# Experts of a two-block network in quads of 32 slots per token tile, on 32-column tiles of TensorE

## The chip, the cores and the metric

One core of one Trainium2 chip runs the whole program once. The metric is the device time of that execution in microseconds (us), the median of several runs. TensorE is called PE, VectorE DVE, ScalarE ACT, GpSimd POOL, and SyncE, whose queue issues the weight loads, SP.

## What is computed

256 tokens of width 1024 pass through two blocks. The first (attention, a short convolution and two feed-forward parts) and the mixing layers of the second are not touched by the change. Each of the two layers of the second block ends in a mixture of experts, which is:

```python
def hier_moe(x, w_group, b_group, w_router, b_router, w_gate, w_up, w_down):
    # N_GROUPS = 4, EXPERTS_PER_GROUP = 4, N_EXPERTS = 16, TOP_K_IN_GROUP = 2, D_EXPERT = 256
    probs_g = jax.nn.softmax((xf @ w_group + b_group).astype(jnp.float32), axis=-1)
    p_top, g_idx = lax.top_k(probs_g, 1)
    ...
    w_top, e_local = lax.top_k(probs_in, TOP_K_IN_GROUP)
    ids = g_idx * EXPERTS_PER_GROUP + e_local
    gates = jnp.einsum('tk,tke->te', p_top * w_top, jax.nn.one_hot(ids, N_EXPERTS, dtype=jnp.float32))
    h = jax.nn.silu(jnp.einsum('td,edf->tef', xf, w_gate)) * jnp.einsum('td,edf->tef', xf, w_up)
    y = jnp.einsum('tef,efd->td', h * gates[:, :, None].astype(h.dtype), w_down)
```

So each token takes the two best experts of its best group, and the result, added to sqrt(2) times the token, goes through a layer normalization.

## The kernel before

**Tokens and weights.** The 256 tokens are two tiles of 128, T = 0 and 1, called T0 and T1 below. All weights are streamed once: `make_plan` lists 512 KB pieces ("units", 128 x 1024 in f32) in the order in which they are used, and SP loads them through a ring of 34 tiles of that size, which also holds the split copies of the dense weights and the larger intermediate tiles (`tS`). A load waits until the last reader of the ring tile that it takes has finished. A layer's experts are 64 units of gate and up weights (`eg`, four per expert) and 32 of down weights (`ed`, two per expert), 96 in all.

**Order.** `Sched` emits the program: every part is a generator that yields the events and estimated times it waits for, and the part that can go on first is emitted next. So each engine's queue holds a fixed order, made from estimated times, and the engines then wait for each other through semaphores.

**An expert layer.** `front_half` transposes a tile and multiplies it with the router's weights. `moe_front` (one call per tile) picks the experts on DVE in some twenty small instructions (`choose`), numbers each expert's tokens by a product with a triangular matrix (the matmul `bk<-mks,cst`), and makes a selection matrix `sel` by comparing with an iota. Its slots are CAP = 64 per expert, counted over both tiles, so 16 x 64 = 1024 columns. A flag is raised if an expert got more than CAP tokens; then a second program (`moe_all`) computes everything again without slots.

`gather` forms the tokens of four experts (256 slots), transposed: per 128 of the 1024 features two tiles of tokens times two parts of a two-part split (`xs`), each a product with 256 columns of `sel`; then `affine` applies the gain and the bias of the normalization, on ACT and DVE by turns. It is called four times.

`moe_task` then goes through the experts in eight pairs, `pr`. `gate_up(pr)` multiplies the 64 slots of each expert of the pair with its gate and up weights (512 columns), in plain f32, the two experts side by side in two 64-column tiles of PE; each such product is two PE instructions in the profile. `slot_gates` (twice) brings the gate of each slot to its partition (`gsl`), and the gate is multiplied into the hidden values. `transposed` turns these, `down(pr-1)` multiplies the previous pair's with its down weights, one bank per half of the 1024 columns, and splits the result `ys` in two parts (ACT cast, DVE subtract). `combine(pr-2)` adds it to the four output banks `out` by products with the transposed selection `selT`: two tiles, two column halves, two parts, so eight products of 512 columns per pair. For pairs 4 and 5 the residual sqrt(2) x is added in the same banks through the identity. `moe` then takes the normalization's statistics from the banks.

Of the kernel before, what the change touches and what calls it, by code (L numbers as in the profile page):

```python
# [22 lines left out]
CAP = 64  # L23
# [7 lines left out]
# ---------------------------------------------------------------- host layout  # L31
# [28 lines left out]
class Plan:  # L60
    """The order in which pieces of the weights are loaded."""
# [11 lines left out]
def make_plan(again=False):  # L73
# [3 lines left out]
    def put(name, kind, n):  # L77
        ids.setdefault(name, [])
        for _ in range(n):
            i = len(ids[name])  # L80
            ids[name].append(p.add(kind, (name, i)))
# [29 lines left out]
    if again:  # L111
        for nm, kd in (moe(0) + lnrows("f0") + [("bin", "dense")] * 20 + [("wo1", "dense")] * 8 + lnrows("m1")
                       + moe(1) + lnrows("f1")):
            put(nm, kd, 1)
        return p, ids
# [20 lines left out]
    for nm, kd in moe(0)[:12] + lnrows("m0") + moe(0)[12:]:  # L136
        put(nm, kd, 1)
# [4 lines left out]
    for nm, kd in moe(1)[:12] + lnrows("m1") + moe(1)[12:]:  # L142
        put(nm, kd, 1)
    for nm, kd in lnrows("f1"):
        put(nm, kd, 1)
    return p, ids


def host_arrays(inp):
# [3 lines left out]
    for i in range(2):  # L153
# [10 lines left out]
        u[f"eg{i}"] = eg.reshape(8, 2, 4, 128, 1024).transpose(0, 2, 1, 3, 4).reshape(64, 128, 1024)  # L164
        ed = np.stack([_down_block(g["w_down_2"][i][e]) for e in range(NEXP)])
        u[f"ed{i}"] = ed.reshape(8, 2, 2, 128, 1024).transpose(0, 2, 1, 3, 4).reshape(32, 128, 1024)
# [62 lines left out]
C_N = 516 + 64  # L229
# [59 lines left out]
class Body:  # L289
# [68 lines left out]
    # ---- estimates of when the vector and scalar engines are done  # L358
# [23 lines left out]
    # ---- small helpers  # L382
# [55 lines left out]
    def mm(self, out, lhsT, rhs, start, stop, shared=False):  # L438
# [72 lines left out]
    # ---- weights  # L511
# [104 lines left out]
    # ---- pieces  # L616
    def setup(self):
# [39 lines left out]
        self.gsl = c.tile([128, 8], F32, name="gsl")  # L657
        self.flag = c.tile([128, 2], F32, name="flag")
# [11 lines left out]
    def gate(self, i):  # L670
        """Until everything before piece i that is not of its own line has been taken."""
# [9 lines left out]
    def ada_task(self):  # L681
        for i in range(2):
            order = [(j, (b,)) for b in range(2) for j in (1, 0)] if i == 0 else [(1, (0, 1)), (0, (0, 1))]
            for j, halves in order + [(j, (0, 1)) for j in (2, 4, 3, 5)]:
# [20 lines left out]
                for b in halves:  # L705
                    d = dst[:, b * 512:(b + 1) * 512] if dst is not None else None
                    if onpe:
                        yield [self.gate(uid[4 * b + 3]), self.unit(uid[4 * b + 3]), self.bk(1)] + ([] if gate else [self.rH(1)])
                        bank = self.bank()
                        for q in range(4):  # L710
                            raw = self.take(uid[4 * b + q]).rearrange("p (k n) -> p k n", k=2)
                            for kk in range(2):
# [3 lines left out]
                                self.sch.now -= 0.22  # L716
# [48 lines left out]
    def gemm(self, T, uids, lhs, blocks, n=512, tail=None, ev=None):  # L765
        """Token-major product of a 128-token tile with streamed weights, one block of columns after another."""
# [29 lines left out]
    def gemm_halves(self, T, uids, lhs, blocks, ev):  # L796
        """As gemm, all the blocks with the first half of the rows before the second half."""
# [21 lines left out]
    def lhsT(self, T, src, out, dst=None, cols=None, at=(0.0, 0.0)):  # L819
        """Transposes [128, 1024] and splits it into two parts, in two halves; cols: a factor and a term per column."""  # L820
# [53 lines left out]
    def residual(self, T, acc, c, g):  # L874
        """x += g * acc on the columns c."""
# [6 lines left out]
    # ---- memory keys and values  # L882
# [46 lines left out]
    def mem_attention(self, T, layer, qm, mm):  # L929
        """qm: [128, 256] on chip. Writes the last two pieces of the mixed tokens, both parts of them."""  # L930
# [54 lines left out]
    # ---- block 1, layer 0  # L985
# [113 lines left out]
    # ---- feed-forward  # L1099
# [52 lines left out]
    # ---- block 1, layer 1  # L1152
# [85 lines left out]
    # ---- block 2  # L1238
# [12 lines left out]
    def residual_half(self, T, b, acc):  # L1251
        """x = alpha x + y on half of the columns, and what its mean and variance take."""
# [13 lines left out]
    def affine_rows(self, T, nm, src):  # L1266
        """x = (src - mean) rstd gain + bias."""
# [13 lines left out]
    def affine_pool(self, T, nm, src):  # L1281
        """The same on the other engines."""
# [534 lines left out]
    def moe_front(self, T, layer):  # L1817
# [29 lines left out]
        if T == 0:  # L1847
            bank = self.bank()
# [357 lines left out]
```

## Time and profile before

| | us |
|---|---|
| median of 3 runs (1238.99 to 1245.82) | 1243.78 |
| span of the profiled execution | 1241.5 |
| PE busy | 1185.2 (95%) |
| DVE busy | 735.7 (59%) |
| ACT busy | 548.4 (44%) |
| mean granted TensorE clock (1 is 2.4 GHz) | 0.980 |
| bytes read from HBM | 299.05 MB, 243 GB/s over the span |

The profiled execution is known by its span, from its first to its last instruction; the median of the runs is 2.3 us longer. Busy shares are averages over stages with different limits. The two expert layers lie at about 824 to 957 us and 1095 to 1228 us of the span, and the stages are read from the views of these stretches. A row of the timeline gives the start, the time from the first start to the last end of merged instructions, engine, line, operation, names, count, and in brackets the idle time before with what ended it.

### The profile page before, as it was taken

What the parts mean: (1) busy time and instruction counts of PE and PEld (TensorE: products, weight loads), DVE (VectorE), ACT (ScalarE), POOL (GpSimd) and SP (SyncE); (2) the same over time, 40 slices, a digit from 0 to 9 for tenths busy, and PEclk for the clock granted to TensorE, in tenths of its full rate; (3) what the DMA queues carried; (4) which work ended last, traced back from release to release, by engine and by line L of the source; (5) the groups of instructions that cost most, each with busy time, mean ns of one, the idle gap of its engine ahead of it and who ended that gap; (6) DMA issues with size and microseconds to landing.
All of it is one profiled execution on the core that took longest, in us unless ns stands there. A gap on an engine that the chain in (4) does not pass through costs nothing. (4 is left out here: it accounts for less than half of the span.)

```text
span 1241.5 us, 15838 instructions
## 1 busy us (share of the span) xinstructions
PE 1185.2 (95%) x5892; PEld 874.0 (70%) x5892; DVE 735.7 (59%) x1177; ACT 548.4 (44%) x912; POOL 45.2 (4%) x60
## 2 busy tenths in 40 slices
PE   7999999999989999999999999989998999899995
PEld 5777778888867887888887798765443786675432
DVE  4477667766768886555657567773313755564213
ACT  4565564534455556433445845422211566422211
POOL 0021000000000000000000001000000100000001
PEclk9999999999999999999999999989999899889998
DMA  9986768677766765556663323857999332487991
GB/s 378 408 283 231 277 219 294 243 260 268 278 229 234 278 228 174 211 208 208 209 211 106 118 86 125 313 206 279 394 408 360 139 133 101 156 325 288 410 409 42
DMA packets 83540, 301.87 MB, mean 243 GB/s; under 512 B 9408, under 2 KB 9824, under 8 KB 83456
## 3 DMA queue, kind: packets, MB, share of 16 engines
q1 hardware_dynamic: 82224, 298.39, 65.9%
q0 software_dynamic: 944, 2.02, 0.5%
q8 instruction: 48, 0.79, 0.3%
q10 hardware_dynamic: 288, 0.38, 0.1%
q14 instruction: 36, 0.29, 0.1%
HBM read 299.05 MB, written 2.10 MB: 243 GB/s over the span
## 5 line engine op out<-in xcount | busy, mean ns | idle before, releaser
L439 PE MATMUL bk<-hi,tS 128*128 128x512 f32 (+1 forms) x1760 | 585.8, 399 | 13.0 <-ACT hi L493 9.4
L439 PEld LDWEIGHTS bk<-hi,tS 128*128 128x128 f32 x1760 | 332.7, 190 | 88.9 <-ACT hi L493 10.0
L474 DVE TENSOR_TENSOR lo<-raw,hi 128x1024 fp32r<-128x1024 f32 x266 | 316.3, 1220 | 54.3 <-ACT hi L493 53.1
L439 PE MATMUL bk<-lo,tS 128*128 128x512 f32 (+1 forms) x880 | 344.5, 391 | 1.8 <-DVE lo L474 1.8
L493 ACT CAST hi<-raw 128x1024 fp32r<-128x1024 f32 x262 | 262.8, 1048 | 6.6 <-DMA raw<-in_units_dram 6.4
L439 PEld LDWEIGHTS bk<-lo,tS 128*128 128x128 f32 x880 | 167.5, 190 | 34.7 <-DVE lo L474 3.1
L467 ACT ACTIVATE tH<-bk 128x256 f32<-128x256 f32 (+1 forms) x94 | 42.2, 451 | 237.2 <-PE bk L439 237.1
L439 PE MATMUL bk<-hi,tH 128*128 128x512 f32 x384 | 132.8, 396 | 0.0
L439 PE MATMUL bk<-raw,tB 128*64 128x512 f32 x384 | 87.0, 602 | 0.0
L439 PEld LDWEIGHTS bk<-hi,tH 128*128 128x128 f32 x384 | 72.5, 189 | 15.0 <-issue 0.2
L474 DVE TENSOR_TENSOR tS<-bk,tS 128x512 fp32r<-128x512 f32 (+2 forms) x58 | 35.9, 633 | 70.2 <-ACT tS L493 68.9
L439 PE MATMUL bk<-raw,tH 128*64 128x512 f32 x320 | 74.5, 597 | 1.2 <-ACT tH L493 1.2
L439 PE MATMUL bk<-lo,tH 128*128 128x512 f32 x192 | 75.0, 391 | 0.0
L493 ACT CAST tS<-bk 128x512 fp32r<-128x512 f32 (+1 forms) x60 | 31.8, 544 | 92.3 <-PE bk L439 72.5
L485 DVE SCALAR_TENSOR_TENSOR tS<-raw,cs,tS 128x1024 f32<-128x1024 f32 x52 | 66.5, 1278 | 0.2
L439 PE MATMUL bk<-tS 128*128 128x256 f32 (+2 forms) x316 | 62.3, 342 | 0.0
L439 PEld LDWEIGHTS bk<-raw,tB 128*64 128x64 f32 x384 | 26.4, 138 | 49.3 <-issue 46.1
L439 PEld LDWEIGHTS bk<-tS 128*128 128x128 f32 x316 | 50.3, 203 | 11.2 <-issue 6.5
L474 DVE TENSOR_TENSOR tH<-tH,bk 128x256 f32<-128x256 f32 x44 | 18.4, 419 | 63.3 <-ACT tH L467 63.2
L451 PE MATMUL bk<-identr,tH 128*128 128x128 f32 x272 | 47.3, 279 | 8.5 <-DVE tH L474 5.9
L451 PEld LDWEIGHTS bk<-identr,tH 128*128 128x128 f32 x272 | 33.8, 141 | 30.3 <-issue 10.5
L493 ACT CAST tH<-bk 128x256 fp32r<-128x256 f32 (+1 forms) x52 | 18.5, 355 | 79.6 <-PE bk L451 75.5
(189 smaller groups left out, 1037.2 us busy)
## 6 DMA issues: line engine op xcount, KB each, us to landing
raw<-in_units_dram SPq DMA_DIRECT2D x556, 512.0 KB, 5.6
row<-in_rows_dram SPq DMA_DIRECT2D x9, 512.0 KB, 6.4
x<-in_x_dram SPq DMA_DIRECT2D x2, 512.0 KB, 8.8
xsave<-x POOLq DMA_DIRECT2D x2, 512.0 KB, 9.1
out_dram<-x SPq DMA_DIRECT2D x3, 256.0 KB, 2.0
ulv<-in_ulv_dram POOLq DMA_DIRECT2D x1, 576.0 KB, 7.2
cst<-in_consts_dram SPq DMA_DIRECT2D x1, 290.0 KB, 9.7
out_dram<-x ACTq DMA_DIRECT2D x1, 256.0 KB, 2.0
```

Of the source, the lines that this page charges most:

```text
L439: self.nc.tensor.matmul(out, lhsT, rhs, start=start, stop=stop, skip_group_check=shared)
L451: self.nc.tensor.transpose(out, in_, self.ident)
L467: self.nc.scalar.activation(out, in_, func, scale=scale)
L474: self.nc.vector.tensor_tensor(out, a, b, op)
L485: self.nc.vector.scalar_tensor_tensor(out, a, s, b, op0, op1)
L493: self.nc.scalar.copy(out, a)
```

## The change

Slots are now counted per tile of tokens: CAP is 32, and `sel` of each tile has 16 x 32 = 512 columns, both tiles side by side in `ulv`. The experts go in four quads `q` instead of eight pairs, and the matmuls of a quad lie on four 32-column tiles, for each tile of tokens apart: `gate_up(q, tiles)` has 8 x 4 products per tile, `down(q, c)` 2 x 2 x 4 for one half `c` of the output columns. `gather` is one call per tile of tokens, with 512 columns and no sum over tiles, and the first quad's `gate_up` is called for T0 and T1 apart, with T1's gather between them. The gates are multiplied into the outputs of `down`, when the two parts are made (ACT copy with a scale, DVE `scalar_tensor_tensor`), and no longer into the hidden values. `combine(q, c)` has four products, since slots of one tile go to that tile alone. The plan's order is 16 units of `eg` and 8 of `ed` in turn, with the down weights laid out by column half. The estimated time of a 32-column matmul in `mm` goes from 0.53 to 0.26 of the full one (0.22 us was taken off by hand before).

```diff
-CAP = 64
+CAP = 32
...
     def moe(i):
-        g, d = [(f"eg{i}", "raw")] * 8, [(f"ed{i}", "raw")] * 4
-        return g + (g + d) * (NEXP // 2 - 1) + d
+        g, d = [(f"eg{i}", "raw")] * 16, [(f"ed{i}", "raw")] * 8
+        return g + (g + d) * (NEXP // 4 - 1) + d
...
-            c = max(0.858 * n / 512, 0.11) * (0.53 if m <= 64 else 1.0)
+            c = max(0.858 * n / 512, 0.11) * (0.26 if m <= 32 and n == 512 else 0.53 if m <= 64 else 1.0)
...
-        sel = self.tS(F32R) if T else self.ulv[:, :1024]
-        self.sel[T] = sel
-        s3 = sel.rearrange("p (e s) -> p e s", e=16)
-        for a, n in ((0, 4), (4, 12)):
-            self.tt(s3[:, a:a + n], p1[:, a:a + n].unsqueeze(2).to_broadcast([128, n, CAP]),
-                    self.cst[:, C_IOTA:C_IOTA + CAP].unsqueeze(1).to_broadcast([128, n, CAP]), ALU.is_equal)
-            if a == 0:
-                self.set(f"rt{layer}_{T}")
+        sel = self.sel[T] = self.ulv[:, T * 512:(T + 1) * 512]
+        self.tt(sel.rearrange("p (e s) -> p e s", e=16), p1.unsqueeze(2).to_broadcast([128, 16, CAP]),
+                self.cst[:, C_IOTA:C_IOTA + CAP].unsqueeze(1).to_broadcast([128, 16, CAP]), ALU.is_equal)
+        self.set(f"rt{layer}_{T}")
...
+        for dk in range(8):
+            yield [self.bk(1 if T else 4), f"rt{layer}_{T}"]
             bank = self.bank()
...
+            for p in range(2):
+                self.mm(bank, self.xs[T][p][:, dk * 128:(dk + 1) * 128], self.sel[T], p == 0, p == 1)
+            self.affine(dk % 2 == 0, self.xg[T][dk], bank, A[:, dk:dk + 1], B[:, dk:dk + 1])
+            self.free()
+            self.set(f"xg{layer}_{T}_{dk}")
+        self.fS(2)
...
+        def combine(q, c):
             for T in range(2):
...
+                if out[T][c] is None:
+                    out[T][c] = self.bank()
+                for p in range(2):
+                    self.mm(out[T][c], self.selT[:, T * 512 + q * 128:T * 512 + (q + 1) * 128],
+                            ys[q, c][p][:, T * 512:(T + 1) * 512], q == 0 and p == 0, q == 3 and p == 1)
...
             self.act(h[:, :256], acc[:, :256], AF.Silu)
-            self.stt(h[:, :256], h[:, :256], gsl[:, pr:pr + 1], acc[:, 256:], ALU.mult, ALU.mult)
...
+            self.tt(h[:, :256], h[:, :256], acc[:, 256:], ALU.mult)
...
+                    for T in tiles:
+                        for e in range(4):
+                            self.mm(acc[T][32 * e:32 * e + 32], self.xg[T][k][:, (4 * q + e) * CAP:(4 * q + e + 1) * CAP],
+                                    ws[e][:, j], k == 0, k == 7)
...
             for j in range(2):
...
+                for T in range(2):
+                    for e in range(4):
+                        self.mm(y[T][32 * e:32 * e + 32], hTs[q][:, T * 256 + j * 128 + 32 * e:T * 256 + j * 128 + 32 * e + 32],
+                                ws[e][:, j * 512:(j + 1) * 512], j == 0, j == 1)
...
+                self.act(ys[q, c][0][:, n], y[T], AF.Copy, scale=g)
+                self.stt(ys[q, c][1][:, n], y[T], g, ys[q, c][0][:, n].bitcast(F32), ALU.mult, ALU.subtract)
...
         yield from self.gather(layer, 0)
...
+        yield from gate_up(0, (0,))
+        yield from self.gather(layer, 1)
+        self.SMIN = SM1
+        yield from gate_up(0, (1,))
+        yield from slot_gates()
+        yield from gate_up(1, (0, 1))
...
+        for q in range(4):
+            if q == 3:
+                self.hold = True
+            yield from down(q, 0)
+            if q > 1:
+                yield from combined(q - 1, 1)
+            yield from down(q, 1)
+            yield from combined(q, 0)
+            if q < 2:
+                yield from gate_up(q + 2, (0, 1))
+            if q == 0:
+                yield from combined(0, 1)
+                yield from residual(0)
+                yield from residual(1)
...
+        yield from combined(3, 1)
```

On PE, at the start of the first expert layer, the order before was as follows. `wr` is the router's product (T1's second half here), `mks` the products that number the tokens, `ulv` and `tS` with 256 columns the gather with T0's and T1's selection, and `raw` the expert weights.

```order
L439 MATMUL bk<-wr,tS 128x20 x4
L439 MATMUL bk<-ulv,tS 128x256 x4
L439 MATMUL bk<-mks,ones 128x16
L439 MATMUL bk<-ulv,tS 128x256 x12
L439 MATMUL bk<-mks,cst 128x16
L439 MATMUL bk<-mks,ones 128x16 x2
L439 MATMUL bk<-tS 128x256 x16
L439 MATMUL bk<-raw,tB 64x512 x12
L439 MATMUL bk<-raw,mkT_117 64x512 x2
L439 MATMUL bk<-raw,tH 64x512 x2
```

In the changed kernel the same place on PE reads:

```order
L452 MATMUL bk<-wr,tS 128x20 x4
L452 MATMUL bk<-ulv,tS 128x512 x16
L452 MATMUL bk<-mks,cst 128x16
L452 MATMUL bk<-raw,tB 32x512 x8
L452 MATMUL bk<-mks,ones 128x16 x2
L452 MATMUL bk<-raw,tB 32x512 x24
L452 MATMUL bk<-ulv,tS 128x512 x6
L464 MATMUL bk<-identr,ulv 128x128 x4
L464 MATMUL bk<-identr,tH 128x128 x2
L452 MATMUL bk<-ulv,tS 128x512 x10
```

A whole first pass over the quad's weights, for T0, now stands ahead of T1's gather; T1's pass over the same weights follows these rows.

On DVE, in the same place, T1's experts were chosen and its selection made before in this order (`mks` is the choice, `tS<-x_83,tS` the second part of T1's split, `tm<-bk,mks` the slot numbers, the two `tS<-tm,cst` T1's selection, and what follows starts the gates):

```order
L474 TENSOR_TENSOR mks<-chosen_88 128x16
L474 TENSOR_TENSOR mks<-mks,chosen_88 128x16
L474 TENSOR_TENSOR tS<-x_83,tS 128x1024
L485 SCALAR_TENSOR_TENSOR tm<-bk,mks 128x16
L474 TENSOR_TENSOR tS<-tm,cst 128x256
L474 TENSOR_TENSOR tS<-tm,cst 128x768
L481 TENSOR_SCALAR tm<-chosen_87 128x4
```

And now:

```order
L487 TENSOR_TENSOR mks<-chosen_88 128x16
L487 TENSOR_TENSOR mks<-mks,chosen_88 128x16
L487 TENSOR_TENSOR tS<-x_83,tS 128x1024
L494 TENSOR_SCALAR tB<-bk,vecs 128x512 x4
L498 SCALAR_TENSOR_TENSOR tm<-bk,mks 128x16
L487 TENSOR_TENSOR ulv<-tm,cst 128x512
L494 TENSOR_SCALAR tm<-chosen_87 128x4
```

DVE's four pieces of T0's gather stand between the choice and the slot numbers of T1.

On PE, the last rows of the first expert layer were (`tH` with `raw` is `down`, `tS` with 512 columns `combine`, `identr,tH` the transposes of hidden values, `tH,cst` and `tH,ones` the next router's):

```order
L439 MATMUL bk<-tS 128x512 x8
L439 MATMUL bk<-raw,tH 64x512 x8
L451 MATMUL bk<-identr,tH 128x128 x2
L439 MATMUL bk<-raw,tH 64x512 x8
L439 MATMUL bk<-tS 128x512 x16
```

and are now:

```order
L464 MATMUL bk<-identr,tH 128x128 x4
L452 MATMUL bk<-raw,tH 32x512 x16
L452 MATMUL bk<-tS 128x512 x4
L452 MATMUL bk<-raw,tH 32x512 x16
L452 MATMUL bk<-tS 128x512 x4
L452 MATMUL bk<-raw,tH 32x512 x16
L452 MATMUL bk<-tS 128x512 x4
L452 MATMUL bk<-raw,tH 32x512 x16
L452 MATMUL bk<-tS 128x512 x8
```

The last two quads' down products, which take 16 units, stand together at the end.

## Rows read from the trace of the kernel before

**Rows 1.** Stretches of both expert layers: busy time of each engine, clock, DMA share, GB/s

```profile
834.40:956.50 122.10, 121.51 (x602) 56.38 (x602) 38.28 (x91) 26.21 (x50) 1.69 (x3) 0.99 0.92 358
1106.10:1227.40 121.30, 120.65 (x601) 55.89 (x600) 37.28 (x88) 26.23 (x50) 0.00 (x0) 1.00 0.79 308
```

**Rows 2.** PE's timeline over one settled pair of experts, first layer

```profile
922.09 0.44 PE L451 MATMUL bk<-identr,tH 128*128 128x128 f32 x2
922.46 5.37 PE L439 MATMUL bk<-raw,tB 128*64 128x512 f32 x24
...
929.48 2.11 PE L439 MATMUL bk<-tS 128*128 128x512 f32 x8
931.52 3.65 PE L439 MATMUL bk<-raw,tH 128*64 128x512 f32 x16
935.10 0.44 PE L451 MATMUL bk<-identr,tH 128*128 128x128 f32 x2
```

**Rows 3.** PE's timeline from the first gather to the second, first layer

```profile
824.38 0.72 PE L439 MATMUL bk<-ulv,tS 128*128 128x256 f32 x4
...
828.66 0.40 PE L439 MATMUL bk<-mks,cst 128*128 128x16 f32 x2 [1.92 <-DVE mks L474]
...
830.76 3.76 PE L439 MATMUL bk<-tS 128*128 128x256 f32 x16
834.45 6.40 PE L439 MATMUL bk<-raw,tB 128*64 128x512 f32 x24
...
842.50 0.28 PE L439 MATMUL bk<-gtr,ulv 128*128 128x32 f32 x1
...
843.41 0.72 PE L439 MATMUL bk<-ulv,tS 128*128 128x256 f32 x4
...
847.27 1.03 PE L451 MATMUL bk<-identr,ulv 128*128 128x128 f32 x8
```

**Rows 4.** PE's timeline: the layers' last combines, and the second layer's start

```profile
952.72 3.93 PE L439 MATMUL bk<-tS 128*128 128x512 f32 x16
...
1093.23 0.96 PE L439 MATMUL bk<-wr,tS 128*128 128x20 f32 x8
...
1106.17 5.37 PE L439 MATMUL bk<-raw,tB 128*64 128x512 f32 x24
...
1223.45 3.92 PE L439 MATMUL bk<-tS 128*128 128x512 f32 x16
```

**Rows 5.** PE's timeline around eight products on 32-column tiles, first block

```profile
24.20 1.92 PE L439 MATMUL bk<-raw,cs 128*32 128x512 f32 x16
26.05 0.50 PE L439 MATMUL bk<-hi,tS 128*128 128x512 f32 x1
```

**Rows 6.** The weight loads into PE (PEld) of these products

```profile
24.65 0.13 PEld L439 LDWEIGHTS bk<-raw,cs 128*32 128x32 f32 x4 [0.30 <-issue]
25.08 0.13 PEld L439 LDWEIGHTS bk<-raw,cs 128*32 128x32 f32 x4 [0.30 <-issue]
```

**Rows 7.** Stretches of 5 us, busy times of instructions on `raw`; last: clock, DMA share, GB/s

```profile
830.00:835.00 5.00, 0.55 (x2) 0.30 (x4) 0.00 (x0) 0.00 (x0) 0.50 0.00 0
...
900.00:905.00 5.00, 2.12 (x10) 0.48 (x8) 0.00 (x0) 0.00 (x0) 1.00 1.03 409
```

**Rows 8.** DMA issues from 830 to 842 us: count, KB each, median us to landing

```profile
raw<-in_units_dram SPq DMA_DIRECT2D x4, 512.0 KB, 4.7
```

**Rows 9.** The page's DMA issues, over the whole span

```profile
xsave<-x POOLq DMA_DIRECT2D x2, 512.0 KB, 9.1
```

**Rows 10.** DVE's timeline in T1's front, first layer

```profile
824.58 0.80 DVE L481 TENSOR_SCALAR x<-x,stat 128x1024 f32<-128x1024 f32 x1
...
828.53 1.22 DVE L474 TENSOR_TENSOR tS<-x,tS 128x1024 fp32r<-128x1024 f32 x1
...
834.48 1.44 DVE L481 TENSOR_SCALAR tB<-bk,vecs 128x256 f32<-128x256 f32 x3
```

**Rows 11.** DVE's timeline after the last combine of the second layer

```profile
1226.05 1.30 DVE L2070 BATCH_NORM_STATS2 tm<-bk 128x6 f32<-128x512 f32 x2 [1.15 <-PE bk L439]
```

More of the change, by code (lines that the diff above doesn't have):

```diff
@@ L657, in setup @@
         self.gsl = c.tile([128, 8], F32, name="gsl")
+        self.gsw = c.tile([128, 2, 32], F32, name="gsw")
+        self.own4 = c.tile([128, 4], F32, name="own4")
+        nc.gpsimd.memset(self.own4, 0.0)
+        for q in range(4):
+            nc.gpsimd.memset(self.own4[32 * q:32 * q + 32, q:q + 1], 1.0)
         self.flag = c.tile([128, 2], F32, name="flag")
@@ L1998, in down, with gate_up @@
-        def down(pr):
-            ud = self.ids[f"ed{layer}"][4 * pr:4 * pr + 4]
-            yield [f"hT{layer}_{pr}", self.rS(2), self.bk(2)]
+            self.set(f"hT{layer}_{q}_{T}")
+        def gate_up(q, tiles):
+            ug = self.ids[f"eg{layer}"][16 * q:16 * q + 16]
+            yield [self.bk(len(tiles)), self.rH(len(tiles))]
+            acc = {T: self.bank() for T in tiles}
+            for k2 in range(4):
+                units = ug[4 * k2:4 * k2 + 4]
+                yield [self.unit(u) for u in units] + ([f"xg{layer}_{tiles[-1]}_{2 * k2 + 1}"] if q == 0 else [])
+                ws = [self.take(u).rearrange("p (k n) -> p k n", k=2) for u in units]
+                for j in range(2):
+                    k = 2 * k2 + j
+                    for T in tiles:
+                        for e in range(4):
+                            self.mm(acc[T][32 * e:32 * e + 32], self.xg[T][k][:, (4 * q + e) * CAP:(4 * q + e + 1) * CAP],
+                                    ws[e][:, j], k == 0, k == 7)
+                    if j == 0:
+                        yield 0.0
+                if tiles[-1] == 1:
+                    for u in units:
+                        self.done(u)
+            for T in tiles:
+                self.sch.spawn(hidden(q, T, acc[T]), 1.9)
@@ L2015, in down, with combined @@
+            if c:
+                self.fH()
+            for T in range(2):
+                n = slice(T * 512, (T + 1) * 512)
+                g = gsl[:, 4 * T + q:4 * T + q + 1]
+                self.act(ys[q, c][0][:, n], y[T], AF.Copy, scale=g)
+                self.stt(ys[q, c][1][:, n], y[T], g, ys[q, c][0][:, n].bitcast(F32), ALU.mult, ALU.subtract)
                 self.free()
-            self.set(f"y{layer}_{pr}")
+            self.set(f"y{layer}_{q}_{c}")
+        def combined(q, c):
+            yield [f"y{layer}_{q}_{c}"] + ([f"selT{layer}_0", f"selT{layer}_1", self.bk(2)] if q == 0 else [])
+            combine(q, c)
@@ new lines, in moe_task @@
+        yield from gate_up(0, (0,))
[4 more added lines that the diff above has]
+        yield from gate_up(1, (0, 1))
+        if layer == 0:
+            self.sch.spawn(self.router(1), 2.5)
+        for q in range(4):
+            if q == 3:
+                self.hold = True
[10 more added lines that the diff above has]
+                yield from residual(1)
@@ L2052, in moe_task @@
         self.fB()
-        yield f"y{layer}_7"
-        self.out = out
-        combine(7)
-        self.fS(2)
+        yield from combined(3, 1)
+        self.fS()
     def moe(self, T, layer):
@@ L2063, in moe @@
         yield from self.moe_front(T, layer)
-        yield f"moe{layer}_{T}"
-        if T == 1 and not self.last[T]:
-            yield lambda: self.tD - 0.3
-        acc = self.out[T]
         st = self.tm(12)
         for b in range(2):
+            yield f"moe{layer}_{T}_{b}"
+            if T == 1 and not self.last[T]:
+                yield lambda: self.tD - 0.3
+            acc = self.out[T]
             self.nc.vector.bn_stats(st[:, 6 * b:6 * b + 6], acc[b])
```

263 lines of the change are left out of this document (94 added, 169 removed).

## The prediction

> **What bounds the kernel now.** I read the stretches first, then PE's timeline, then the loads and DVE in the places that the change touches. Over the expert part of each layer PE is busy for 121.5 of 122.1 and 120.7 of 121.3 us, at a clock of 0.99 and 1.00, while DVE and ACT are busy for 38 and 26 us of it [rows 1]. A busy PE need not be at its pace, so look at one settled pair: `gate_up` takes 922.46 to 929.48, 7.02 us for 32 instructions (0.219 each), combine 2.04, `down` 3.58, the transposes 0.37, and the next pair follows at once [rows 2]. So PE sets the pace. The second limit is close behind: from 900 us the loads move 409 GB/s at a DMA share of 1.03 [rows 7], so a unit of 0.524 MB costs 1.28 us. A pair takes 12 units, 15.4 us of loads, in 13.0 us of PE: PE lives on what was loaded ahead. The loads stand still at 830 to 835 us (0 GB/s, the ring is full), where the clock is also at 0.50, its 1.2 GHz level [rows 7], after PE had waited 1.92 us for DVE's choice of T1's experts [rows 3].
>
> **The change part by part.**
>
> *The products themselves: no gain.* A pass for one tile of tokens over a quad has 32 products, 64 instructions. The eight 32-column products of the first block take 1.85 us for 16 instructions with both edges, 0.116 each [rows 5], and their weight loads come four per 0.43 us, 0.108 each [rows 6]. I take 0.108 and 0.1 us for a group's edges: 6.9 us for a pass, 3.6 for the 32 instructions of a `down`. Per layer that is 8 x (6.9 + 3.6) = 84 us, where 8 x (7.02 + 3.58) = 85 were. The bounds are 0.108 and 0.219 (the pace of 64 columns, if no more than two tiles ran at once); I stay at the row that has 32-column tiles.
>
> These rows show four tiles at once. The Trainium skill, "TensorE: Matmul & The Clock Gate", Measured speedup vs the span model, gives 2.38 times for three 32-column tiles, and its section The mechanism lets weight loads overlap running matmuls only where the row group differs, which is not so here. By 2.38 of 3 an instruction would take 0.108 x 3 / 2.38 = 0.136 us, an estimate from that page, and the layer 21 us more. The row decides.
>
> *Gather.* Four calls of 3.86 us [rows 3], 15.4, become 32 products of 512 columns at the combine's 0.24 (3.93 for 16, [rows 4]): 7.7. *Combine.* Eight of 2.04 become eight of four products, 1.0 each: 8.3 us less. *Slot gates* are made once, 0.9 us less [rows 3], and half of sixteen transposes goes, 0.9 of about 1.9. So PE has about 18 us less per layer. Scaling outputs instead of hidden values costs nothing on the path: ACT and DVE stand idle two thirds of the time [rows 1], and each handles 16 halves of 512 columns per layer as before.
>
> *T1's front: PE is filled, DVE is later.* T0's selection has half the columns, so DVE's chain for T1 starts some 0.6 us sooner (half of the 1.22 us of 1024 elements, [rows 10]) and the split ends at 829.1, not 829.7. Then four pieces of T0's gather stand ahead of T1's slot numbers in DVE's queue. A piece of 256 columns takes 0.48 (1.44 for three, [rows 10]); for 512 it is between that and 0.96, and I take 0.70, near the statistics of 512 columns in 0.65 [rows 11]. So T1's numbers wait 2.8 us, to 831.9, and its selection is there at 832.8. Queued behind are the gates, and PE's second gather waits. But PE has the first pass meanwhile: from the first of these pieces, 829.9, to 837.1 with the numbering products. Second gather and six transposes, 4.5, and edges: T1's pass begins at 841.9. In the second layer I count from the router's first half at 1093.23 [rows 4]: both router halves 1.9, transposes 0.5, gather 3.8, pass 6.9, numbering 0.3, gather 3.8, transposes 0.7, and an estimated 1.2 of waits for DVE's last pieces, which stand behind T1's choice: 1112.3. Before, the first pair began at 834.45 and 1106.17 [rows 3, 4].
>
> *PE from T1's pass to the end.* Pass 6.9, gates and transposes 1.6, quad 1 13.9, two downs with transposes and a combine 8.7, quad 2 with the next router's products 14.4, combine and transposes 1.5, residual 2.0 and about 1.5 of waiting for its parts (two scaled copies and two subtractions of 1024 columns), downs and combine 8.2, quad 3 13.9, 1.5 for its hidden values, which no other work now covers, four downs 14.4 and three combines 3.0, the last splitting and combines 2.1. Sum 93.6: PE alone would end at 935.5 and, without the router, 1205.4.
>
> *The loads.* In the built order 27 units and the two rows of a normalization are placed before T0's gather, two more behind it, units 29 and 30 (from 0) wait for T1's gather, and 31 on for T1's pass, sixteen ring tiles in 7 us. So from 841.9 on the loads never wait for the ring: unit 29 lands 4.7 us later (a load into an idle queue, [rows 8]) and each further one after 1.28. The last, 95, lands at 841.9 + 4.7 + 66 x 1.28 = 931.1; the two 512 KB of `xsave` in the first layer [rows 9] take 2.6 of the same DMA: 933.7. The last `down` and the last splitting, 5.7, end at 939.4. In the second layer 1112.3 + 4.7 + 84.5 + 5.7 = 1207.2. Both are later than PE alone, by 3.9 and 1.8: **the loads become the bound, narrowly.** Before, the ends were 956.65 and 1227.37 [rows 4]. Gains 17.2 and 20.2.
>
> *Tails.* Before, T0's statistics began 1.3 us ahead of PE's last combine (1226.05 against 1227.37, [rows 4, 11]), since T0's four products came first. Now the last half of both tiles comes last and DVE has its splitting to finish first: about 1 us lost in each layer.
>
> Sum: 17.2 + 20.2 - 2 = 35.4, so a span of about 1206 for the 1241.5 of the profiled execution. The median of the runs is 2.3 above that span: **1208 us**.
>
> **The rivals.**
>
> *Loads come later still.* SP issues in order, so one ring tile freed late holds all units behind it: two units of the third quad wait for DVE's last use of the normalization's rows, and several for combines. For it: quad 3 and the last downs use 32 units in 33 us of PE, where the loads need 41. Against: by then the queue is many units behind its free tiles. If about 6 units are lost in each layer, 12 x 1.28 = 15 us: 1223.
>
> *PE stays the bound.* If the pieces on DVE are cheaper or T1's pass starts 3 us sooner, the loads restart sooner too; if besides the two loads of `xsave` fall in a gap, the ends come at 934 and 1203: 9 to 11 us less, 1198.
>
> *Four column tiles do not run four at once with real weights.* In the rows the weights are one column repeated 32 times and eight products long; here each product has weights of its own and its streams come from four ring tiles. This ends on the other side. There are 768 such instructions in a layer; each 0.01 us more costs 7.7 there, of which the loads hide 3.9 and 1.8. The gain of 35.4 is gone at (35.4 + 5.7) / 1536 = 0.027 more, 0.135 us an instruction. At 0.136, the page's figure above, it is 1244, no change; at 0.219 it is 1208 + 170 - 6 = 1372. Against: the rows show four loads per 0.43 us without a gap.
>
> *It doesn't do what it says:* a tile with more than 32 tokens of an expert would run the second program, at least 220 units, 282 us more. From the given inputs the greatest count I work out is 28.
>
> **How the numbers follow.** Forecast 0.60 (1202 to 1214, the unknown pieces on DVE and the waits of the residual), later loads 0.15, PE the bound 0.14, column tiles short of four 0.10 (half of it within 0.5% of no change or a little on either side), the second program 0.01. The range reaches from below the second case to above the first of the rivals, 1195 to 1226. About 0.5%, 6 us, is what a measurement can tell from no change. Faster 0.91, same 0.03, slower 0.06.
>
> **What would show it.** T1's pass at about 842 - 834.5 = 7.5 us behind the place of the old first pair (6 in the second layer); a pass of 64 instructions in 6.9 us and a `down` in 3.6; PE's clock at 1.00 through T1's front, where it was 0.50; loads at 409 GB/s without a gap from there to the last unit; PE waiting for `raw` in quad 3 and the last downs, a few us in all. Wrong would be: a pass over 8 us, a gap in the loads after T1's pass, or an expert part (from the old place of the first pair) longer than 110 us.

## The result, and the profile after

The changed kernel takes **1207.26 us** (median of 4 runs, 1206.49 to 1210.04) where the kernel before, beside it on the same chip, takes 1243.01: a ratio of 0.9719, 95% interval 0.9692 to 0.9746. Two later sets of five gave 1208.01 (0.9713, 0.9688 to 0.9739) and 1208.24 (0.9724, 0.9693 to 0.9755). The profiled execution has a span of 1204.7 us.

First the stretches of the first layer's front, then both expert layers whole, from T0's gather (first layer) and from the router (second) to the end of the last combine. Columns: length, busy time of PE, PEld, DVE, ACT, POOL, clock, DMA share, GB/s.

```profile
827.00:832.00 5.00, 4.74 (x43) 1.82 (x46) 4.69 (x16) 1.86 (x2) 0.00 (x0) 1.00 0.63 213
832.00:837.00 5.00, 5.00 (x40) 2.17 (x33) 2.23 (x11) 1.16 (x2) 0.00 (x0) 1.00 0.00 0
837.00:842.00 5.00, 5.00 (x36) 2.83 (x38) 2.79 (x4) 3.08 (x5) 0.00 (x0) 1.00 0.22 70
842.00:847.00 5.00, 5.00 (x50) 1.47 (x42) 0.00 (x0) 0.00 (x0) 0.00 (x0) 1.00 0.99 350
...
860.00:915.00 55.00, 53.85 (x451) 18.46 (x444) 16.17 (x28) 9.94 (x19) 1.09 (x2) 1.00 1.03 410
```

```profile
821.71:938.31 116.60, 113.85 (x884) 44.34 (x883) 40.10 (x99) 27.54 (x48) 1.60 (x3) 0.99 0.92 363
1075.13:1189.95 114.82, 112.63 (x899) 44.08 (x897) 40.87 (x97) 28.00 (x49) 0.55 (x1) 1.00 0.92 367
```

The ring is still full at 832 to 837 us (0 GB/s, as in [rows 7]), but PE works through it at full clock. The loads restart there, and from 847 us to the end of the layer they run at 407 to 415 GB/s in every stretch of 5 to 10 us, without a gap. PE is busy for 113.9 of 116.6 us, no longer for all of it as in [rows 1].

PE's timeline in the first layer: start, length, operation, count, idle time before and its releaser.

```profile
821.71 5.51 PE L452 MATMUL bk<-ulv,tS 128*128 128x512 f32 x16
827.06 0.29 PE L452 MATMUL bk<-mks,cst 128*128 128x16 f32 x2
827.28 1.92 PE L452 MATMUL bk<-raw,tB 128*32 128x512 f32 x16
829.47 0.62 PE L452 MATMUL bk<-mks,ones 128*128 128x16 f32 x4 [0.26 <-DVE tm L498]
830.02 5.36 PE L452 MATMUL bk<-raw,tB 128*32 128x512 f32 x48
835.30 1.66 PE L452 MATMUL bk<-ulv,tS 128*128 128x512 f32 x6
...
839.83 3.64 PE L452 MATMUL bk<-raw,tB 128*32 128x512 f32 x32
...
846.84 0.62 PE L452 MATMUL bk<-gtr,ulv 128*128 128x32 f32 x4
848.30 0.62 PE L452 MATMUL bk<-gtr,ulv 128*128 128x32 f32 x4 [0.84 <-DVE gsw L487]
```

```profile
912.16 0.62 PE L452 MATMUL bk<-raw,tB 128*32 128x512 f32 x1 [0.24 <-DMA raw<-in_units_dram]
912.16 0.63 PE L452 MATMUL bk<-raw,tH 128*32 128x512 f32 x3
...
921.95 4.07 PE L452 MATMUL bk<-raw,tH 128*32 128x512 f32 x32
925.95 1.19 PE L452 MATMUL bk<-tS 128*128 128x512 f32 x4
927.07 4.07 PE L452 MATMUL bk<-raw,tH 128*32 128x512 f32 x32
...
936.17 2.14 PE L452 MATMUL bk<-tS 128*128 128x512 f32 x8
```

T1's pass is 839.83 to 846.84, 7.01 us for 64 instructions, 0.1095 each. Its place is 18.1 us behind the start of T0's gather. A `down` of 32 instructions in the last quad takes 4.07, and from the start of one `down` to the start of the next it is 5.12, which is 4 x 1.28: the pace of four loads. PE alone needs 3.64 for such a `down` and 4.70 for the period (the run without the stores, below). The waits hardly show as idle time: they show as rows of 4.07 where 3.64 would do.

T0's gather takes 5.51 us here, at a granted clock of 0.50 (822 to 825 us). In the two repeats of this kernel the clock was 1.00 and the gather took 3.88 and 3.93, with the same two waits ahead of it, 0.65 and 0.68. T1's pass still began 18.1 us behind the start of T0's gather in all three, since in the repeats PE waited 0.40 and 1.17 us for DVE instead. From one of them:

```profile
822.03 3.88 PE L452 MATMUL bk<-ulv,tS 128*128 128x512 f32 x16
```

In the second layer the same rows read

```profile
1075.13 0.96 PE L452 MATMUL bk<-wr,tS 128*128 128x20 f32 x8
...
1081.14 2.78 PE L452 MATMUL bk<-raw,tB 128*32 128x512 f32 x24
...
1093.85 3.64 PE L452 MATMUL bk<-raw,tB 128*32 128x512 f32 x32
...
1100.85 0.62 PE L452 MATMUL bk<-gtr,ulv 128*128 128x32 f32 x4
```

```profile
1183.83 4.06 PE L452 MATMUL bk<-raw,tH 128*32 128x512 f32 x32
1187.82 2.13 PE L452 MATMUL bk<-tS 128*128 128x512 f32 x8
```

The gain of 36.8 us of span is made of these parts. The first layer, from T0's gather to the end of the last combine: 132.3 (824.38 to 956.65, [rows 3, 4]) to 116.6, 15.7 less. The second, from the router's 0.96 us row: 134.1 (1093.23 to 1227.37, [rows 4]) to 114.8, 19.3 less. What stands between the layers and behind the second: 0.9 more. And 2.7 us were won before the first gather, where the two programs issue the same work. That last part does not come from the change, as the third run of it shows below.

### The profile page after: what moved, and what is told of

It reads as the page before. It is cut to its first block, busy times and chain, and to the rows that moved or that the text cites. A ratio compares the mean times of both kernels' runs of the same rounds, so it can differ in the third digit from the quotient of the medians.

```text
span 1204.7 us, 16681 instructions
## 1 busy us (share of the span) xinstructions
PE 1146.4 (95%) x6368; PEld 829.1 (69%) x6368; DVE 722.4 (60%) x1111; ACT 545.0 (45%) x894; POOL 46.2 (4%) x65
## 5 line engine op out<-in xcount | busy, mean ns | idle before, releaser
L487 DVE TENSOR_TENSOR tH<-tH,bk 128x256 f32<-128x256 f32 x60 | 25.2, 420 | 149.4 <-ACT tH L480 149.3
L452 PE MATMUL bk<-raw,tB 128*32 128x512 f32 x768 | 92.2, 594 | 0.2 <-DMA raw<-in_units_dram 0.2
L452 PE MATMUL bk<-raw,tH 128*32 128x512 f32 x640 | 78.9, 594 | 0.0
L452 PEld LDWEIGHTS bk<-raw,tB 128*32 128x32 f32 x768 | 24.6, 110 | 53.6 <-issue 47.0
L498 DVE SCALAR_TENSOR_TENSOR tS<-bk,gsl,tS 128x512 fp32r<-128x512 f32 x32 | 23.7, 750 | 53.5 <-ACT tS L480 47.7
L452 PEld LDWEIGHTS bk<-raw,tH 128*32 128x32 f32 x640 | 22.3, 110 | 44.9 <-issue 38.1
L487 DVE TENSOR_TENSOR tH<-bk,tH 128x256 fp32r<-128x256 f32 (+1 forms) x52 | 20.8, 400 | 46.1 <-ACT tH L506 46.1
L506 ACT COPY tH<-bk 128x512 f32<-128x512 f32 (+1 forms) x50 | 23.9, 486 | 51.6 <-PE bk L452 37.1
```

Of the source, the lines that this page charges most:

```text
L452: self.nc.tensor.matmul(out, lhsT, rhs, start=start, stop=stop, skip_group_check=shared)
L487: self.nc.vector.tensor_tensor(out, a, b, op)
L498: self.nc.vector.scalar_tensor_tensor(out, a, s, b, op0, op1)
L506: self.nc.scalar.copy(out, a)
```

## The experiments

All times are medians of 4 or 5 executions (2 for the pairs on one column tile, 12 for the kernel before with more transfers). The runs were made on several chips; each ratio is to the kernel before beside the run on its chip. "Layer 1" and "layer 2" are the lengths from the start of T0's gather to the end of the last combine, read from PE's timeline of each profiled execution; "start" is where that first gather begins. (In the second layer of the kernel before, T0's gather stood behind both halves of the router, so its 130.6 is short by some 3 us against the others.)

| kernel | time, us | ratio to before, 95% | start | layer 1 | layer 2 |
|---|---|---|---|---|---|
| before | 1243.0 | | 824.4 | 132.3 | 130.6 |
| changed | 1207.26 | 0.9719 (0.9692, 0.9746) | 821.7 | 116.6 | 114.0 |
| changed, again | 1208.01 | 0.9713 (0.9688, 0.9739) | 822.0 | 115.8 | 113.3 |
| changed, third time | 1208.24 | 0.9724 (0.9693, 0.9755) | 824.1 | 116.3 | 114.2 |
| without the stores of x | 1204.96 | 0.9688 (0.9662, 0.9715) | 826.7 | 113.4 | 113.5 |
| four more transfers per layer | 1217.49 | 0.9790 (0.9764, 0.9817) | 822.3 | 121.7 | 118.7 |
| before, four more transfers | 1243.34 | 1.0017 (1.0000, 1.0033) | 824.4 | 132.3 | 130.4 |
| half the combine | 1209.01 | 0.9730 (0.9705, 0.9756) | 824.7 | 115.8 | 113.2 |
| combine twice | 1219.41 | 0.9798 (0.9782, 0.9813) | 821.8 | 123.2 | 122.3 |
| pairs on one column tile | 1207.30 | 0.9727 (0.9692, 0.9762) | 821.7 | 116.3 | 113.1 |
| first quad in one pass | 1219.16 | 0.9801 (0.9777, 0.9825) | 827.0 | 121.2 | 119.1 |
| one pass, T0's pieces on ACT | 1210.10 | 0.9751 (0.9728, 0.9775) | 821.7 | 117.0 | 116.0 |
| half pass | 1204.99 | 0.9684 (0.9665, 0.9702) | 826.7 | 113.3 | 113.3 |
| half pass, again | 1206.67 | 0.9704 (0.9672, 0.9737) | 826.8 | 113.4 | 113.3 |

My theory: the loads end both layers, narrowly, and PE would end them a little sooner. The rival: PE still ends them, and the loads are hidden.

**The changed kernel, twice more.**

> The changed kernel once more, as the measure of the runs beside it. Its profiled run had 36.8 us less span than the kernel before, and 2.7 of them were there already at the first gather. If that lead is of the change, this profile has its first gather at 821.7 us again; if it is the spread between runs, the gather lies anywhere from 821 to 825, with the time behind it unchanged.

> The changed kernel beside the half-pass version on one chip, to measure the small difference between the two. Expected as before, 1207 to 1208 us, 116 us from the start of T0's gather to the end of the last combine in the first layer and 113 to 114 in the second.

The first gather began at 822.0 and 824.1 us, in one program. The third run has the start of the kernel before (824.4) and a clock of 0.98 in the stretch from 100 to 200 us and again from 300 to 400, as the kernel before has; the first profile had 1.00 in both. So the 2.7 us are spread between executions. The lengths of the layers in these three profiles agree within 0.8 and 0.9 us, which is what a difference below must exceed.

**Less to move: no stores of x.**

```diff
-        if nm == "m0":
-            self.nc.gpsimd.dma_start(self.xsave[T], x)
...
-            self.nc.sync.dma_start(self.x[T], self.xsave[T])
+            self.nc.sync.dma_start(self.x[T], self.x_d[T])
```

> Leaves out the two 512 KB stores of x for the second program (a second program would start from the input). They are issued at 878 and 880 us in the first expert layer. Loads theory: 1 MB at 410 GB/s is 2.56 us of the same DMA, so the units of the last down products land 2.6 us sooner: the first expert layer ends 1.6 to 2.6 us sooner (1.6 if PE's own work ends it), the second is the same: -1.6 to -2.6 in all. PE theory: 0.

Layer 1 fell by 2.4 to 3.2, layer 2 by no more than identical layers differ. PE's timeline of this run in the last quad of the first layer, and its last `down` of the second:

```profile
924.89 3.64 PE L452 MATMUL bk<-raw,tH 128*32 128x512 f32 x32
...
934.31 3.64 PE L452 MATMUL bk<-raw,tH 128*32 128x512 f32 x32
...
1184.20 4.07 PE L452 MATMUL bk<-raw,tH 128*32 128x512 f32 x32
```

In the first layer every `down` is at PE's own 3.64 again. A transfer that nothing waits for had lengthened the layer, and 113.4 is what PE alone needs in layer 1. In the second layer, where nothing was left out, the loads still set the pace.

**More to move, in both kernels.**

```diff
...
+            if not self.again and self.plan.src[i] in (("eg0", 40), ("eg1", 40)):
+                for j in range(4):
+                    self.nc.sync.dma_start(self.spare[4 * int(self.plan.src[i][0][2]) + j], self.units_d[j])
+                    self.dma_t += 1.46
```

> Four further transfers of 512 KB from device memory to device memory on the loads' queue in each expert layer, in the middle of the units (at the first unit of the second half of gate_up); nothing waits for them. Loads theory: 4 x 1.28 = 5.1 us in each layer, all of it in the end, +10 in all (more if such a copy takes more of the DMA than a load). PE theory: PE is hidden behind nothing and the loads have slack, 0 to +2 in all.

> The kernel before with the same four transfers of 512 KB more in each expert layer that cost the changed kernel 5 to 6 us per layer. Loads theory of the change (the old kernel is bound by PE, its loads have slack at the end of each layer): 0, at most +1 in all. If the four transfers cost the old kernel the same 10 us, then they act through something else than the bound (contention, the ring), and the run on the changed kernel shows nothing of its bound.

The changed kernel lost 9.5 us (1217.49 to 1208.01), 5.5 in layer 1 (against the mean of its three profiles, 116.2) and 4.9 in layer 2 (113.8), for an expected 5.1 each. The kernel before lost nothing that can be measured. Where its slack was is to be seen in the stretch at the end of its second layer, without and with the transfers:

```profile
1210.00:1228.00 18.00, 16.75 (x74) 7.53 (x70) 5.13 (x10) 3.00 (x6) 0.08 (x1) 1.00 0.04 18
```

```profile
1210.00:1228.00 18.00, 16.31 (x72) 7.39 (x68) 5.57 (x11) 3.00 (x6) 0.52 (x1) 1.00 0.33 134
```

Before, the DMA stood idle there (0.04), and the loads that the four transfers had pushed back went into that time. The bound has changed hands.

**Less and more for PE.**

```diff
# half the combine
-                for p in range(2):
+                for p in range(1):
...
-                            ys[q, c][p][:, T * 512:(T + 1) * 512], q == 0 and p == 0, q == 3 and p == 1)
+                            ys[q, c][p][:, T * 512:(T + 1) * 512], q == 0, q == 3)
# combine twice
-                for p in range(2):
+                for n, p in enumerate((0, 0, 1, 1)):
...
-                            ys[q, c][p][:, T * 512:(T + 1) * 512], q == 0 and p == 0, q == 3 and p == 1)
+                            ys[q, c][p][:, T * 512:(T + 1) * 512], q == 0 and n == 0, q == 3 and n == 3)
```

> Of each combine only the products with the first of the two parts of the outputs are issued, 32 products of 0.25 to 0.27 us less in each expert layer, but 4 of them (1.1 us) stand behind the last units of a layer. The result leaves the second, small part of the expert outputs out. It is the changed kernel with 8 us less of PE's work per layer and the same loads. Loads theory (units of the last down products land last; 2.4 us of slack on PE in the first layer, about none in the second): only what stands behind the last units is saved, -1.1 in each layer, -2 to -3 in all. PE theory: -4 in each layer, -8 in all.

> Each combine product is issued twice, so the expert outputs enter the result doubled: 32 products of 0.25 to 0.27 us more for PE in each layer, 8 us, the same loads. It measures how far PE is from being the bound. Loads theory (PE 2.4 us ahead in the first layer and 0.5 to 1.5 in the second): +5.6 and +6.5 to +7.5, +12 to +13 in all. PE theory: +16 in all.

What I expected of half the combine had its size wrong: a layer has 32 combine products in all, so 16 go, 3.6 us of PE and not 8 (six rows from 1.19 to 0.73, the last from 2.14 to 1.35). It gave nothing in all, not even what it saved behind the last unit (0.8 us). PE's timeline of that run:

```profile
923.80 0.73 PE L452 MATMUL bk<-tS 128*128 128x512 f32 x2
924.46 4.53 PE L452 MATMUL bk<-raw,tH 128*32 128x512 f32 x32
...
944.03 1.09 PE L464 MATMUL bk<-identr,x 128*128 128x128 f32 x4 [3.53 <-DVE x L498]
```

The combine shrank from 1.19 to 0.73 and the `down` behind it grew from 4.07 to 4.53: the period stays 5.12. What was saved behind the last unit came back as a longer wait for DVE, 3.53 where the changed kernel has 2.74. The second layer has the same 5.12. So the loads bound both layers, and DVE what follows.

Combine twice adds 7.3 us of combine products per layer (six combines from 1.19 to 2.11, the last from 2.14 to 3.94). It also brought what I had not expected, a longer stop at the residual and half clock behind it. In the first layer PE's rows and the stretch with the clock (columns as in the stretches above) read:

```profile
891.74 0.73 PE L452 MATMUL bk<-tS,identr 128*128 128x512 f32 x2 [1.47 <-ACT tS L480]
...
895.29 7.99 PE L452 MATMUL bk<-raw,tH 128*32 128x512 f32 x64
...
937.44 3.64 PE L452 MATMUL bk<-raw,tH 128*32 128x512 f32 x32
941.01 3.94 PE L452 MATMUL bk<-tS 128*128 128x512 f32 x16
```

```profile
894.00:897.00 3.00, 3.00 (x13) 0.90 (x15) 0.08 (x1) 0.00 (x0) 0.00 (x0) 0.50 1.03 411
```

From the transposes ahead of the residual to the next `down` it is 5.6 us where the changed kernel has 4.0, and the two `down` behind it take 7.99 for 7.07; the second layer has the same stop, and 8.09. Together that is 2.5 and 2.6 us. Layer 1 rose by 6.9 and layer 2 by 8.4. The whole rose by 11 to 12 by the medians, and by 13.0 by the spans of this profile and the first one, which both have their gather at 821.7 or 821.8: behind the layers 1.9 us came back. That this lies near the expected 12 to 13 is in part luck, since the products cost less than the 8 us assumed and the stop was not priced. Every `down` of the last quads is 3.64, so PE alone ends these layers. Taking off the 7.3 and the stop gives PE's own end in the changed kernel: 123.2 - 7.3 - 2.5 = 113.4 in the first layer, as in the run without the stores, and 122.3 - 7.3 - 2.6 = 112.4 in the second. So the loads end the first layer 2.4 to 3.2 us behind PE's own end, and the second 0.9 to 1.8.

**Which products run side by side.**

```diff
-                    for T in tiles:
-                        for e in range(4):
+                    for e in range(4):
+                        for T in tiles:
```

> The same products of gate_up, but in quads 1 to 3 the two token tiles are the inner loop: two neighbouring instructions write the same column tile (of two accumulators), then two the next. Theory (four instructions run at once only where the next three in PE's order go to other column tiles): the second of each pair waits for the first, so two run at once instead of four, 0.11 becomes about 0.22 us for 384 instructions of a layer: +41 us per layer, +80 in all. Rival (any four instructions share the array, whatever their order, or PE has queues per tile): 0.

The rival won: no change. A stretch of the pass in quad 1 of this run:

```profile
849.54 8.00 PE L452 MATMUL bk<-raw,tB 128*32 128x512 f32 x72
857.29 1.11 PE L452 MATMUL bk<-raw,mkT 128*32 128x512 f32 x8
858.15 1.11 PE L452 MATMUL bk<-raw,tB 128*32 128x512 f32 x8
```

72 instructions in 8.00 us, 0.11 each, though two neighbouring products always share a column tile; with neighbours on different tiles 72 take 7.93. Four tiles are busy at once either way, and the order within such a group of eight products is free. The trace also shows which half of the rival it is. In this stretch `mkT` holds tokens of T1 and `tB` those of T0, and the program issues a product of one and of the other in turn, two instructions each; yet eight instructions of the one start, and then eight of the other, as in the changed kernel. So instructions did not start in the order of the program, and queues per column tile fit that. The Trainium skill, "TensorE: Matmul & The Clock Gate", The mechanism, has products start and end strictly in program order; by that the second product of a pair would hold back the next pair's first, and the pace would be that of two tiles. This run does not agree with it.

**Is the pass between the gathers worth its late loads?**

```diff
-        yield from gate_up(0, (0,))
         yield from self.gather(layer, 1)
         self.SMIN = SM1
-        yield from gate_up(0, (1,))
+        yield from gate_up(0, (0, 1))
```

> The first quad's gate_up is issued once for both token tiles behind both gathers, so PE has nothing between the two gathers. Loads theory (the last down products wait for loads, which restart only when T1's pass reads the ring): T1's one-hot is there at 830.2, so its gather starts 5 us sooner and the loads restart 5 us sooner; PE is 2 us later into quad 1 (both passes from 834.9 on, 13.9 us). The waits for raw in quad 3 vanish, PE ends each layer alone: -2.3 to +0.4 us in each layer, about -1 in all. Rival (PE is the bound, and filling the bubble was the gain): nothing is given back, +2 in each layer, +4 in all. The order of the old kernel kept for the first quad would then be worth that much.

Both theories missed: +11 us, 5.0 in layer 1 and 5.2 in layer 2. PE's timeline around T1's gather in the second layer, the clock in it, and then the residual products of the first layer:

```profile
1093.87 0.40 PE L452 MATMUL bk<-mks,cst 128*128 128x16 f32 x2 [2.11 <-DVE mks L487]
1096.52 1.04 PE L452 MATMUL bk<-mks,ones 128*128 128x16 f32 x4 [2.26 <-DVE tm L498]
1097.40 6.09 PE L452 MATMUL bk<-ulv,tS 128*128 128x512 f32 x16
```

```profile
1098.00:1102.00 4.00, 4.00 (x11) 3.13 (x10) 3.62 (x17) 1.55 (x2) 0.00 (x0) 0.50 0.71 282
```

```profile
899.93 0.73 PE L452 MATMUL bk<-tS,identr 128*128 128x512 f32 x2 [0.95 <-ACT tS L480]
901.19 1.22 PE L452 MATMUL bk<-tS,identr 128*128 128x512 f32 x2 [0.53 <-DVE tS L498]
902.34 9.62 PE L452 MATMUL bk<-raw,tH 128*32 128x512 f32 x64
```

I had priced an idle time of 2 us and nothing for the clock. In the second layer PE waited 2.11 and 2.26 us, the granted clock was then 0.50, the 1.2 GHz level, and the gather took 6.09 instead of 3.9. Both passes there ended 5.9 us later than in the changed kernel (30.8 against 24.9 behind T0's gather), though T1's gather began 2.4 sooner: the waits are 4.4 us of what was lost there, the slower gather 2.2. In the first layer the front cost 2.7; there the new order brought a second stop, at the residual, and the two `down` behind it took 9.62 where they take 7.07. The units did come sooner and no longer held the last quad, but PE's own end had moved behind them.

```diff
 (first quad in one pass, as above)
-            self.affine(dk % 2 == 0, self.xg[T][dk], bank, A[:, dk:dk + 1], B[:, dk:dk + 1])
+            self.affine(T == 0 or dk % 2 == 0, self.xg[T][dk], bank, A[:, dk:dk + 1], B[:, dk:dk + 1])
```

> The first quad's gate_up once for both tiles behind both gathers, as in the run that had +11 us, and besides all eight pieces of T0's gather are scaled on ACT, so that DVE makes T1's one-hot at once. T1's gather then starts about 6 us behind T0's start (8.6 and 10.9 in that run, 13.6 in the changed kernel), PE has no bubble in which its clock falls, and both passes end 24 to 25 us behind the start of T0's gather, as in the changed kernel; the loads restart 6 us sooner. Loads theory: -2.4 in the first layer, -0.5 in the second, -3 in all. Rival (ACT's pace of 0.73 us per piece holds the gathers, the bubble and the half clock come back): +3 to +6 in each layer, as without the change on ACT.

It gave +2, between the two. DVE, free of T0's pieces, let T1's gather start 6.6 us behind T0's in the first layer (828.30 behind 821.67), and the passes ended at 25.0, as in the changed kernel, with the units early. But both residues of the run above were left:

```profile
891.78 0.74 PE L452 MATMUL bk<-tS,identr 128*128 128x512 f32 x2 [0.95 <-ACT tS L480]
...
894.14 8.24 PE L452 MATMUL bk<-raw,tH 128*32 128x512 f32 x64
...
1084.79 5.22 PE L452 MATMUL bk<-ulv,tS 128*128 128x512 f32 x16
```

The stop at the residual and the slow `down` behind it in the first layer, a gather of 5.22 us in the second.

**Half a pass.** What remains is to fill the bubble and no more.

```diff
...
-        yield from gate_up(0, (0,))
+        yield from gate_up(0, (0,), (0, 1))
         yield from self.gather(layer, 1)
         self.SMIN = SM1
-        yield from gate_up(0, (1,))
+        yield from gate_up(0, (1,), (0, 1))
+        yield from gate_up(0, (0, 1), (2, 3))
```

(the third argument names the blocks of the contraction; the accumulators of T0 stay open.)

> The first quad's pass of T0 is cut in two: its first half (32 products, 3.5 us) stays between the gathers, where PE waits for T1's one-hot, and its second half goes behind T1's gather, together with T1's. In the trace of the changed kernel T1's one-hot is there at 830.2 us and its gather starts only at 835.3, behind the whole pass; here it starts near 831, so the loads restart 4 us sooner, and PE has the same work and no bubble. Loads theory: the waits for units go, -2.4 in the first layer (what leaving out the stores gave), -0.5 to -1.5 in the second, -3 to -4 in all. Rivals: DVE, with the gate numbers of both tiles ahead of T1's pieces, holds T1's gather and gives it back: 0; or the order of x and the residual products falls as in the two runs that issued the pass once, with a stop of 0.95 us and half clock behind it: +1 in the first layer, 0 in all.

> The half-pass version once more. Theory (PE ends each layer, its waits for units gone): 113.3 us from the start of T0's gather to the end of the last combine in both layers, 2.5 us less than the changed kernel in the first, 0 to 0.5 in the second, about 1205 us. Rival (its 1205.0 came from the spread between runs): 1207 to 1208, as the changed kernel.

```profile
836.84 3.92 PE L452 MATMUL bk<-ulv,tS 128*128 128x512 f32 x16
840.69 4.50 PE L452 MATMUL bk<-raw,tB 128*32 128x512 f32 x40
...
920.16 3.64 PE L452 MATMUL bk<-raw,tH 128*32 128x512 f32 x32
...
1086.83 0.62 PE L452 MATMUL bk<-mks,ones 128*128 128x16 f32 x4 [0.73 <-DVE tm L498]
1087.64 3.91 PE L452 MATMUL bk<-ulv,tS 128*128 128x512 f32 x16 [0.20 <-DVE tm L494]
```

In the first layer T1's gather starts 10.2 us behind T0's (13.6 in the changed kernel), at full clock, and in both layers every `down` is PE's 3.64. Layer 1 is 113.3 in both runs, 2.4 to 3.3 below the three profiles of the changed kernel; layer 2 is 0.1 above to 0.9 below, no more than identical layers differ. There PE waits 0.73 and 0.20 us for DVE ahead of T1's gather, and quad 1 starts 28.5 us behind T0's gather where the changed kernel has 27.6, so most of what the sooner loads gave went back. By the medians its second run is 1.6 us faster than the changed kernel beside it, and its first 3 us faster than the changed kernel's earlier repeat on another chip; the intervals overlap, so the gain is shown for the first layer's length and not for the whole time. It has PE as its bound, so nothing more is to be had from sooner loads.

## Why the prediction was right, step by step

The forecast was 1208 and its likeliest case happened, for the reason given: the loads became the bound, narrowly. That the medians of 1207.3 to 1208.2 lie within 1 us of it is in part luck: the terms below missed by 1 to 2 us in both directions, and the start of the first gather alone differs by 2.4 us between executions of this kernel.

- *Four column tiles at once.* 0.108 was taken, 0.1095 measured, 7.01 for a pass of 6.9. By the Trainium skill, "TensorE: Matmul & The Clock Gate", Measured speedup vs the span model, three tiles give 2.38 times, and an instruction would have been 0.136 (an estimate from that page); the trace does not agree, and four tiles ran at twice the pace of the two before (0.219, [rows 2]). The rival that ended on the other side rested on real weights being worse than the first block's; they are not.
- *T1's front.* DVE's four pieces of T0's gather took 2.96 us, 0.74 each for the 0.70 assumed, and T1's pass began 18.1 us behind T0's gather for 17.5, and 18.7 behind the router for 19.1. The clock was 1.00 from 827 us on, as said; that it was 0.50 at 822 to 825 us in the first profile was not said, and cost nothing. The run with one pass adds what the prediction did not say: the pass in the bubble is worth 5 us a layer, the waiting that it fills and the clock that it keeps up taken together.
- *The loads.* No gap, four units per 5.12, so no ring tile that came free late held them up. Layer 1 ended 115.8 to 116.6 behind T0's gather for a predicted 115.0, and layer 2 114.1 to 115.0 behind the router for 114.0.
- *PE alone.* This term was too small by 2.3 us in layer 1 and about 1 in layer 2: 111.1 behind T0's gather predicted, 113.4 shown without the stores; 112.2 behind the router predicted in layer 2, 113.2 worked out from the run with the combine twice (112.4 behind T0's gather, which starts 0.8 later). The slot gates make 1.1 of it in each: 2.7 us from their first product to quad 1, with 0.84 and 0.78 of waiting for DVE between the tiles, where 1.6 was put for them and the transposes. So the margin of the loads, 3.9 and 1.8 in the prediction, is 2.4 to 3.2 and 0.9 to 1.8.
- *Tails.* 2 us were put, 0.9 measured: 0.6 of it behind the second layer.
- *The sum* was 35.4. Without the 2.7 us of an earlier start, the profiles differ by 34.1, and the medians by 35.7.

## What to carry to other kernels

Work moved into an engine's bubble can be worth more than the idle time it fills, when the clock would fall to half behind the bubble, as it did here. But fill only the bubble: what goes in beyond it holds back whatever is queued behind, here the loads. When a change moves one limit close to the second, an added cost that nothing waits for (a store, an extra copy) shows which limit is at work, and the same addition in the old kernel is its control. A row that is longer than its instructions need can hide waits that are not listed. And read the clock before taking an added cost at its face value: the run with the combine twice had 2.5 us of stop and slower clock on top of its 7.3 us of products.

## What the runs showed of the hardware

- Products in pairs on the same column tile ran as fast as with neighbours on different tiles: 72 instructions in 8.00 us against 7.93. I had expected the second of a pair to wait. The instructions started in another order than the program's. The changed kernel shows the same where a load is late: at 912.16 us one instruction on `tB` and three of the next group, on `tH`, start together, behind a wait of 0.24 us for a unit.
- A copy from device memory to device memory on the loads' queue cost as much as a load: 5.5 and 4.9 us for four, 1.2 to 1.4 each, beside loads of 1.28.
- The clock before the expert part differs between executions of one program. In the three profiles of the changed kernel it is 0.98 in one or in two of the stretches of 100 us up to 500 us and 1.00 in the rest, and the first gather begins at 822 or 824 us; in other runs with the same work ahead of the experts it is 0.97 in two stretches, and the gather begins at 827.
- In the run with one pass, waits of 0.53, 0.95 and 0.53 us close together at the residual were followed by a clock of 0.50 (902 to 906 us), and the two `down` behind them took 2.5 us more; with the combine twice, waits of 1.47 and 0.53 were (894 to 897 us). Waits of 0.52 and 0.39 in the changed kernel at the same place left it at 1.00. The waits alone do not decide it: behind the same waits of 0.65 and 0.68 ahead of T0's gather the clock was 0.50 in one profile of the changed kernel and 1.00 in two.
